# A block of three token mixers on one core: eighteen chunks of x's projections by Strassen's product, memory attention moved beside the forgetting attention's values

## The chip, the core and the metric

The kernel runs on one core of one Trainium2 chip. The metric is the device time in microseconds (us); lower is better. The engines are called as the profile calls them: PE is TensorE's matmul, DVE VectorE, ACT ScalarE, POOL GpSimd, SP the engine that issues most of the DMAs.

## The reference

One layer on x of 1024 tokens x 1024 channels in fp32. All three mixers read one combined projection of the normalised x.

```python
h = rmsnorm(x, norm_mix_g)
z = h @ w_in                                   # hq hf hi hg | fq fk fv ff | mq | 3 x 1024 gate logits
y_a = hgrn2(hq, hf, hi, hg)                    # 4 heads of 128, gated recurrence, norm per head
y_b = fox(fq, fk, fv, ff)                      # 8 heads of 64, causal attention with log-forget bias
mem_kv = rmsnorm(mem) @ mem_kv_w               # 256 memory tokens
y_c = memory(mq, mem_kv)                       # 4 heads of 128: softmax(q k') v over 256 tokens
g = sigmoid(gate_logits)                       # one gate per channel and branch
merged = g0 * (y_a @ w_br_hgrn) + g1 * (y_b @ w_br_fox) + g2 * (y_c @ w_br_mem)
x = x + merged @ w_out
a, v = split(rmsnorm(x) @ w_up)                # 2 x 2816
x = x + (gelu(causal_conv3(a) + b) * v) @ w_down
```

The square sum of a token's channels scales a whole column of x, so the kernel multiplies the raw, gain-scaled x into the weights and applies 1/rms afterwards (`rx`, the row spread over 128 partitions, or `rt`, a column per 128 tokens).

## The kernel before, in words

Data lie channel-major: a tile is 128 channels x 1024 tokens. Every large product is made of fp32r parts: an operand is cast to a high part (`uh`, `wh`, usually on ACT, L115) and the difference is the low part (`ul`, `wl`, on DVE, L123); `mm3` (L109 to L111) issues three matmuls, high x high, high x low, low x high. PSUM has eight banks of 512 columns: three named `pp` for projections, two `lg` for logits, two `tr` for transposes, one `po` for attention's sums.

The stages, in the order of time: the front (keys and values of memory, x loaded chunk by chunk and split, the first two gate chunks, the norm of x); the values of the forgetting attention (`fox_values`) and the projections of its first head pair (`fox_proj(0)`); its eight heads, two per pair p, while projections of the next pair and gate chunks are woven between; the HGRN values, preparation and mix per head; memory attention with its own projections; the three branches' output projections with the gates (`gates`); w_out; the up-projection, made by Strassen's product in units of two 128-channel chunks (84 matmuls of 512 columns where 96 would do it directly); the down-projection.

A chunk (`cm_chunk`) is 128 output channels by 1024 tokens: 48 matmuls of 512 columns. 28 such chunks are concerned here, 24 of gate logits and four of the memory's queries `mq`. A gate chunk ends in a product with `rx` on DVE (L373), a tanh on ACT (L374) and a store to memory (`gd`), from where the branches read it back. How many gate chunks are woven beside which head stands in two tables:

```python
NGF = [0, 3, 1, 2, 0, 5, 2, 0]     # beside the eight heads of the forgetting attention
NG = [1, 1, 0, 3, 0, 0, 0, 3]      # beside four HGRN heads and four memory heads
```

`weave` takes steps of several generators in turn, by the share of their steps done; `ahead` gives attention a higher priority. From that a planner writes a fixed order for each engine, with its own estimate of times; each engine then runs its list strictly in order and waits where an operand is late.

In one attention head a block of 128 queries goes through logits (PE into `lg`), a fused bias and row maximum (DVE L527), exponential (ACT L537), reciprocal (DVE L538), scaling (POOL L539), transposes (PE L550 to L553 into `tr`), the split of the transposed block (ACT L115, DVE L123: `ph`, `pl`), and the products with the values (PE L562, L563 into `po`). The end of an HGRN head's half (L727 to L749) is: `po`, its square on ACT (L741), the sum on DVE (L742), the power on POOL (L128), scaling on ACT (L745), four transposes (L748), the output `ya` on DVE (L749).

## Time and profile before

| | |
|---|---|
| median of 3 runs | 1778.67 us (1777.25 to 1780.26) |
| the profiled execution | 1779.33 us, its span from first to last instruction 1777.6 us |
| granted clock of PE | 0.997 |
| PE, DVE, ACT, POOL busy | 1755.8, 1146.1, 731.0, 359.9 us |

By stages, in us of the span, busy time of PE, DVE and ACT:

| stage | from - to | PE | DVE | ACT |
|---|---|---|---|---|
| front | 0 - 66 | 53.0 | 52.3 | 31.4 |
| values, first projections | 66 - 136 | 70.0 | 16.7 | 22.9 |
| forgetting attention | 136 - 510 | 374.0 | 225.1 | 193.0 |
| HGRN | 510 - 787 | 277.0 | 200.2 | 108.2 |
| memory attention | 787 - 884 | 97.0 | 46.6 | 44.8 |
| branches | 884 - 1020 | 136.0 | 77.6 | 26.3 |
| w_out | 1020 - 1128 | 108.0 | 64.0 | 47.8 |
| up-projection | 1128 - 1558 | 427.1 | 335.7 | 185.5 |
| down-projection | 1558 - 1777 | 213.8 | 127.9 | 71.2 |

Lines of a timeline give the start, the busy time, engine, line of the kernel, operation, output and inputs, shape, and in brackets the idle time before it with what ended it. Lines of groups end in busy time, mean duration of one in ns, and idle time before them with its causes. Busy times of neighbours overlap, since instructions are pipelined: how far two starts lie apart is the price of one.

### The profile page before, as it was taken

Reading aid. Unit: us, or ns where it says so; the run is one execution under the profiler, and the core shown is the slowest. Engines: PE = TensorE matmul, PEld = TensorE weight load, DVE = VectorE, ACT = ScalarE, POOL = GpSimd, SP = SyncE. Lnnn points to the kernel's source line nnn. Section 1 sums busy time; section 2 is a strip of 40 time slices with the busy share of each in tenths; the row PEclk is TensorE's granted clock in tenths of the full one; section 3 lists DMA queues with packets and bytes.
Section 4 is the critical chain, followed back from the end, with each engine's and each line's share of the span. In section 5 each row is a group of like instructions: output and inputs, shape, how many; then the busy total and the mean of one; then the engine's idle time right before and its main releaser. Section 6 shows DMA issues by size and latency. Waiting matters only on the chain.

```text
span 1777.6 us, 24366 instructions
## 1 busy us (share of the span) xinstructions
PE 1755.8 (99%) x9173; PEld 1487.1 (84%) x9173; DVE 1146.1 (64%) x2070; ACT 731.0 (41%) x1215; POOL 359.9 (20%) x430
## 2 busy tenths in 40 slices
PE   7999999999999999999999999999999999999999
PEld 5899899889988888888888888788888888778887
DVE  8436665565657778735446665787877877775654
ACT  4336454444544344314521143543433444433332
POOL 5214334342223333323100000111111111100000
PEclk9999999999999999999999999999999999999999
DMA  7212221221211111130144442455545444394782
GB/s 265 98 61 70 70 69 62 73 88 60 69 50 43 42 48 34 45 125 25 54 142 142 148 166 84 142 165 173 154 132 158 124 125 140 135 371 144 232 281 83
DMA packets 75573, 208.45 MB, mean 117 GB/s; under 512 B 8752, under 2 KB 11576, under 8 KB 75328
## 3 DMA queue, kind: packets, MB, share of 16 engines
q1 hardware_dynamic: 60864, 154.99, 25.2%
q0 software_dynamic: 14592, 51.91, 10.3%
q8 instruction: 72, 1.18, 0.3%
q14 instruction: 45, 0.37, 0.1%
HBM read 168.82 MB, written 61.12 MB: 129 GB/s over the span
## 4 chain that ended last, share of the span: by engine, by line
PE 96%; issue 1%; DMA 1%; DVE 1%; POOL 1%; ACT 0%; SPq 0%; DVEq 0%; POOLq 0%
PE pp L110 21%; PE pp L111 21%; PE pp L109 21%; PE lg L110 4%; PE lg L111 4%; PE lg L109 4%; PE tr L109 2%; PE tr L110 2%; PE tr L111 2%; PE lg L696 2%; PE po L563 1%; PE lg L522 1%; PE po L562 1%; PE lg L521 1%; PE po L110 1%
## 5 line engine op out<-in xcount | busy, mean ns | idle before, releaser
L111 PE MATMUL pp<-uh,wl 128*128 128x512 f32 x608 | 243.6, 401 | 0.0
L110 PE MATMUL pp<-ul,wh 128*128 128x512 f32 x608 | 243.2, 400 | 0.0
L109 PE MATMUL pp<-uh,wh 128*128 128x512 f32 x608 | 241.7, 397 | 0.0
L110 PE MATMUL pp<-wl,uh 128*128 128x256 f32 (+1 forms) x512 | 144.9, 283 | 0.0
L111 PE MATMUL pp<-wh,ul 128*128 128x256 f32 (+1 forms) x512 | 144.6, 283 | 0.0
L109 PE MATMUL pp<-wh,uh 128*128 128x256 f32 (+1 forms) x512 | 143.9, 283 | 0.0
L115 ACT CAST wh<-raw 128x1024 fp32r<-128x1024 f32 (+2 forms) x80 | 73.1, 914 | 153.0 <-PE pp L110 123.3
L109 PEld LDWEIGHTS pp<-uh,wh 128*128 128x128 f32 x608 | 115.3, 190 | 23.3
L110 PEld LDWEIGHTS pp<-ul,wh 128*128 128x128 f32 x608 | 114.5, 188 | 22.9
L111 PEld LDWEIGHTS pp<-uh,wl 128*128 128x128 f32 x608 | 114.4, 188 | 22.5
L1074 POOL DMA_DIRECT2D rw<-in_w_up x44 | 24.3, 559 | 463.8 <-DVE wl L123 410.8
L123 DVE TENSOR_TENSOR wl<-raw,wh 128x1024 fp32r<-128x1024 f32 (+2 forms) x87 | 93.9, 1081 | 29.7 <-ACT wh L115 23.0
L115 ACT CAST wh<-s 128x512 fp32r<-128x512 f32 x85 | 51.9, 619 | 125.6 <-PE pp L110 60.7
L110 PEld LDWEIGHTS pp<-wl,uh 128*128 128x128 f32 x512 | 96.4, 188 | 0.9
L111 PEld LDWEIGHTS pp<-wh,ul 128*128 128x128 f32 x512 | 96.5, 189 | 0.6
L109 PEld LDWEIGHTS pp<-wh,uh 128*128 128x128 f32 x512 | 96.2, 189 | 0.7
L115 ACT CAST dwh<-wr 128x1024 fp32r<-128x1024 f32 (+1 forms) x42 | 41.1, 980 | 124.7 <-PE tr L110 41.7
L115 ACT CAST wh<-rw 128x512 fp32r<-128x512 f32 x65 | 40.0, 620 | 86.1 <-PE pp L110 48.3
L123 DVE TENSOR_TENSOR dwl<-wr,dwh 128x1024 fp32r<-128x1024 f32 (+1 forms) x42 | 47.6, 1133 | 38.7 <-ACT dwh L115 37.5
L677 POOL TENSOR_TENSOR X<-X,kt 128x256 f32<-128x256 f32 x48 | 48.2, 1011 | 109.9 <-ACT X L676 109.9
L539 POOL TENSOR_SCALAR pt<-pt,st 128x128 f32<-128x128 f32 (+3 forms) x64 | 57.0, 891 | 62.4 <-DVE st L538 50.5
L537 ACT ACTIVATE pt<-pt,st 128x128 f32<-128x128 f32 (+3 forms) x64 | 49.7, 777 | 35.1 <-DVE st L534 29.0
(426 smaller groups left out, 4845.1 us busy)
## 6 DMA issues: line engine op xcount, KB each, us to landing
rw<-in_w_up POOLq DMA_DIRECT2D x44, 512.0 KB, 4.7
raw<-in_w_cm SPq DMA_DIRECT2D x40, 512.0 KB, 3.5
sd<-in_w_dn POOLq DMA_DIRECT2D x30, 512.0 KB, 6.1
br<-yd SPq DMA_DIRECT2D x30, 512.0 KB, 5.4
gd<-gt SPq DMA_DIRECT2D x46, 256.0 KB, 2.0
gt<-gd SPq DMA_DIRECT2D x46, 256.0 KB, 2.7
...
```

The costliest lines, as they stand in the source:

```text
L109: PE.matmul(ps, lh, rh, start=first, stop=False, skip_group_check=more)
L110: PE.matmul(ps, lh, rl, start=False, stop=False, skip_group_check=more)
L111: PE.matmul(ps, ll, rh, start=False, stop=last, skip_group_check=more)
L115: S.copy(out, in_)
L123: return (sub or V).tensor_sub(l, src, h.bitcast(F32))
L521: PE.matmul(ps[:, :w], qa[i][:, tsl], kh[i][:, s0:s0 + w], start=True, stop=False)
L522: fox_sets[p][3] = PE.matmul(ps[:, :w], qa[i][:, tsl], kl[i][:, s0:s0 + w], start=False, stop=True)
L537: S.activation(pt[:, :ns], pt[:, :ns], AF.Exp, bias=st[:, 2:3], accum_out=st[:, 3:4])
L539: G.tensor_scalar(pt[:, :ns], pt[:, :ns], st[:, 3:4], 0.0, ALU.mult, ALU.add)
L677: G.tensor_mul(Xk, Xk, Kv[:, :, 0, :])
L696: PE.matmul(o[:, b * 64:(b + 1) * 64], X[:, b * P:(b + 1) * P], Xq[:, b * bpb:(b + 1) * bpb, :], start=True, stop=True)
L1074: late["raw"] = G.dma_start(raw[:, 2 * i:2 * i + 2, :], src[:, 2 * i:2 * i + 2, :])
```

## The change

18 of the 28 chunks (the four of `mq` and 14 of the gates) are made right after the front, in nine pairs, by Strassen's product in Winograd's form: seven products of quarter size, 84 matmuls instead of 96 per pair. For that, x is read again from memory in eight loads (`rows`), scaled by the norm's gain on ACT, and sums of its quarters are split into four families T1 to T4 (`differences`), the other three operands being quarters of the parts of x that exist (B11, B21, B22). The pairs' weights come as a new input `w_pair` through POOL's queue. Two plain gate chunks (NCOVER) run before. `rx` is spread behind the last of the row loads. The results of `mq` go to memory.

Memory attention now reads them and is woven beside `fox_values` and `fox_proj(0)`; its output parts go to memory (`ycd`) and come back before the third branch. Beside the heads of the forgetting attention six gate chunks are left, two beside the second head of each of the first three pairs (NFOX). Beside the first three HGRN heads only the next head's preparation is woven, beside the last the branch of the forgetting attention (`branch(1)`); then follow the branches of HGRN and of memory. Sums and parts of the branches lie in the place of x's parts.

```diff
-NGF = [0, 3, 1, 2, 0, 5, 2, 0]
-NG = [1, 1, 0, 3, 0, 0, 0, 3]
-NPRE = 2 + sum(NG) + sum(NGF)
+ORDER = [(br, j) for br in (1, 0, 2) for j in range(8)]
+NCOVER, NPAIR, NFOX = 2, 14, 2
+
+_dense = [12, 13, 14, 15] + [16 + 8 * br + j for br, j in ORDER[4:4 + NPAIR]]
+PAIRS = list(zip(_dense[0::2], _dense[1::2]))
+assert 2 + NCOVER + NPAIR + 3 * NFOX == len(ORDER) and len(_dense) % 2 == 0
...
+    early = iter([i for i in range(2, len(order)) if i < 2 + NCOVER or i >= 2 + NCOVER + NPAIR])
+
+    def gates_early(count):
+        for _ in range(count):
+            i = next(early)
+            br, j = order[i]
+            for n, ps in cm_chunk(w_cm[16 + 8 * br + j], KC, uh, ul):
+                SP.dma_start(gd[i, n], gate(n, ps))
+                yield
...
+    def block(b, k):
+        if b in fam:
+            return [t[:, k, :] for t in fam[b]]
+        c, n = int(b[1]) - 1, int(b[2]) - 1
+        return [t[k + 4 * c][:, n * HB:(n + 1) * HB] for t in (uh, ul)]
+
+    def product(ps, op, b, first):
+        wh, wl = op
+        for k in range(4):
+            ks = slice(k * P, (k + 1) * P)
+            bh, bl = block(b, k)
+            mm3(ps, wh[:, ks], wl[:, ks], bh, bl, first and k == 0, k == 3, not first)
...
+        def snap(self, ps):
+            e = ps1.tile([P, HB], F32, tag="fe", name="fe", bufs=3)
+            S.copy(e, ps)
+            return e
...
+    def dense_unit(src, put, first, families):
+
+        raw = []
+        whole = None if first else dense.raw()
+        for i in range(2):
+            if first:
+                t = wp.tile([P, 4 * 264], F32, tag="raw", name="raw", bufs=2)[:, :2 * HB]
+                t = t.rearrange("p (a b) -> p a b", a=2)
+            else:
+                t = whole[:, 2 * i:2 * i + 2, :]
+            G.dma_start(t, src[:, 2 * i:2 * i + 2, :])
+            raw += [t[:, 0, :], t[:, 1, :]]
+        a11, a21, a22, a12 = raw
+        x, y = ps_proj(), ps_lg()
+        o1 = dense.operand(a11)
+        if first:
+            o6 = dense.operand(a12)
+        s1 = dense.sum_of(1, a21, a22)
+        o2 = dense.operand(s1)
+        s2 = dense.sum_of(2, s1, a11)
+        product(x, o1, "B11", True)
+        e1 = dense.snap(x)
+        if first:
+            z = ps_tr()
+            product(z, o6, "B21", True)
+            put(0, 0, z, e1)
+            next(families)
+        product(y, o2, "T1", True)
+        e5 = dense.snap(y)
+        product(x, dense.operand(s2), "T2", False)
+        e2 = dense.snap(x)
+        run_all(families)
+        s4 = dense.sum_of(4, s2, a12)
+        product(y, dense.operand(s4), "B22", False)
+        put(0, 1, y, e2)
+        s3 = dense.sum_of(3, a11, a21)
+        product(x, dense.operand(s3), "T3", False)
+        put(1, 1, x, e5)
+        if not first:
+            z = ps_tr()
+            product(z, dense.operand(a12), "B21", True)
+            put(0, 0, z, e1)
+        product(x, dense.operand(a22), "T4", False)
+        put(1, 0, x, None)
...
+            if e is not None:
+                V.tensor_add(t, ps, e)
+            src = ps if e is None else t
+            if c:
+                V.scalar_tensor_tensor(out=t, in0=src, scalar=-1.0, in1=rx[:, sl], op0=ALU.mult, op1=ALU.mult)
+            else:
+                V.tensor_mul(t, src, rx[:, sl])
+            S.activation(t, t, AF.Tanh, scale=0.5)
+            SP.dma_start(gd[order.index(divmod(ch - 16, 8)), n], t)
...
+    for k, t in enumerate(rows):
+        t = t.rearrange("p (c n) t -> p c (n t)", c=2)
+        for c in range(2):
+            last_row = SP.dma_start(t[:, c, :], xT[:, k + 4 * c, :])
+    with tc.issue_after(last_row.ins):
+        spread_dma(rx, rt, cp, "rx")
...
+    def differences():
+
+        b = []
+        for k, t in enumerate(rows):
+            t = t.rearrange("p (c n) t -> p c (n t)", c=2)
+            for c in range(2):
+                S.activation(t[:, c, :], t[:, c, :], AF.Copy, scale=col(C_GX + k + 4 * c))
+            b.append([t[:, c, n * HB:(n + 1) * HB] for c in range(2) for n in range(2)])
+        for k, (b11, b12, b21, b22) in enumerate(b):
+            V.tensor_sub(b11, b11, b12)
+            family_block("T1", k, b11)
+        yield
+        order_after = ExitStack()
+        order_after.enter_context(tc.issue_after(first_gates.ins))
+        for k, (t1, b12, b21, b22) in enumerate(b):
+            V.scalar_tensor_tensor(out=t1, in0=t1, scalar=-1.0, in1=b22, op0=ALU.mult, op1=ALU.subtract)
+            family_block("T2", k, t1)
...
+    cover, families = gates_early(NCOVER), differences()
+    next(cover)
+    next(families)
+    run_all(cover)
+    next(families)
+    for i, chunks_of in enumerate(PAIRS):
+        dense_unit(w_pair[i], dense_put(chunks_of), i == 0, families)
+    ps1.release()
+    fam.clear()
...
+    def mem_prep(h):
+        mqh = pm.tile([P, T], F32R, tag="mqh", name=f"mqh_{h}", bufs=2)
+        mql = pm.tile([P, T], F32R, tag="mql", name=f"mql_{h}", bufs=2)
+        rq = pm.tile([P, 8], F32, tag="rq", name=f"rq_{h}", bufs=2)
+        t = pm.tile([P, T], F32, tag="mqf", name=f"mqf_{h}", bufs=2)
+        SP.dma_start(t, mqd[h])
...
+            for t, d in zip(yt, ycd):
+                SP.dma_start(d[:, h, n * HB:(n + 1) * HB], t.bitcast(F32))
+            yield
+
+    def memory():
+        run_all(mem_prep(0))
+        yield
+        for h in range(4):
+            if h < 3:
+                run_all(mem_prep(h + 1))
+            yield from mem_attn(h)
...
-    run_all(fox_values())
+    weave((chain(fox_values(), fox_proj(0)), 25), (ahead(memory(), AHEAD), 4 * MEM_STEPS))
     small_consts()
-    run_all(fox_proj(0))
+    pm.release()
+    pf = pools["pf"] = tc.alloc_tile_pool(name="pf", bufs=1, side="right", reuse_waits="tile")
+    mskf = pf.tile([P, P], F32, tag="mskf", name="mskf")
+    SP.dma_start(mskf, mats[:, 2 * P:3 * P])
     fox_prep(0)
     for p in range(3):
-        weave((ahead(fox_attn(p, 0), AHEAD), FOX_STEPS), (fox_proj(p + 1), 8),
-              (gates_early(NGF[2 * p]), 2 * NGF[2 * p], FOX_LATE))
+        weave((ahead(fox_attn(p, 0), AHEAD), FOX_STEPS), (fox_proj(p + 1), 8))
         fox_prep(p + 1, fox_sets[p][3])
-        weave((ahead(fox_attn(p, 1), AHEAD), FOX_STEPS),
-              (gates_early(NGF[2 * p + 1]), 2 * NGF[2 * p + 1], FOX_LATE))
+        weave((ahead(fox_attn(p, 1), AHEAD), FOX_STEPS), (gates_early(NFOX), 2 * NFOX, FOX_LATE))
...
-        weave((ahead(fox_attn(3, i), AHEAD), FOX_STEPS), (islice(values, 8), 8),
-              (gates_early(NGF[6 + i]), 2 * NGF[6 + i], FOX_LATE))
+        weave((ahead(fox_attn(3, i), AHEAD), FOX_STEPS), (islice(values, 8), 8))
...
-        weave((ahead(hgrn_mix(h, ya), AHEAD), HGRN_STEPS), (hgrn_prep(h + 1), 6), (gates_early(NG[h]), 2 * NG[h]))
-    weave((ahead(hgrn_mix(3, ya), AHEAD), HGRN_STEPS), (gates_early(NG[3]), 2 * NG[3]))
+        weave((ahead(hgrn_mix(h, ya), AHEAD), HGRN_STEPS), (hgrn_prep(h + 1), 6))
...
+    yh, yl = [[place(p, 2 + c, f"y{p}{c}") for c in range(4)] for p in "hl"]
+    for c in range(4):
+        t = place("hl"[c % 2], c // 2, f"yb{c}", F32)
+        SP.dma_start(t, ybd[:, c, :])
+        split(S, yh[c], yl[c], t)
...
+    weave((ahead(hgrn_mix(3, ya), AHEAD), HGRN_STEPS), (branch(1, yh, yl), 16))
+    state["ph"].release()
+    pv.release()
+    for c in range(4):
+        split(S, yh[c], yl[c], ya[:, c, :])
+    py = tc.alloc_tile_pool(name="py", bufs=1, side="right", reuse_waits="tile")
+    yc = [[py.tile([P, T], F32R, tag=f"yc{p}{c}", name=f"yc{p}{c}") for c in range(4)] for p in "hl"]
+    for c in range(4):
+        for t, d in zip(yc, ycd):
+            G.dma_start(t[c], d[:, c, :].bitcast(F32R))
+    run_all(branch(0, yh, yl))
+    run_all(branch(2, *yc))
```

How the planner's order changes is shown at three places. Line numbers behind the change are about 280 higher in the attention and HGRN. The first is ACT at the end of the front; `rx_row` is the row of 1/rms, `Vf` the attention's values. Before:

```order
L115 CAST wh_763<-raw_761 128x1056
L276 COPY rx_row_499<-tr_497 8x128
L420 ACTIVATE Vf_529<-pp_553,rt_88 128x256
L420 ACTIVATE Vf_529<-pp_579,rt_88 128x256
L374 ACTIVATE gt_510<-gt_510 128x512
L374 ACTIVATE gt_514<-gt_514 128x512
L374 ACTIVATE gt_518<-gt_518 128x512
L420 ACTIVATE Vf_529<-pp_605,rt_88 128x256
```

Now, with `xrT4h`, `rw`, `xrT4l` the row tiles, `T1h` the high part of family T1, `s1`, `s2` sums of the first pair's weights:

```order
L119 CAST wh_722<-raw_716 128x512
L119 CAST wh_722<-raw_718 128x512
L280 COPY rx_row_535<-tr_533 8x128
L548 ACTIVATE xrT4h_512<-xrT4h_512,cv_64 128x1024 x2
L119 CAST T1h_516<-xrT4h_512 128x512
L548 ACTIVATE rw_514<-rw_514,cv_64 128x1024 x2
L119 CAST T1h_516<-rw_514 128x512
L548 ACTIVATE xrT4l_513<-xrT4l_513,cv_64 128x1024 x2
L119 CAST wh_730<-s1_728 128x512
L119 CAST wh_730<-s2_734 128x512
L119 CAST T1h_516<-xrT4l_513 128x512
L548 ACTIVATE rw_515<-rw_515,cv_64 128x1024 x2
```

Where the values' evictions and the gates' tanh stood behind the copy of `rx_row`, eight scales of rows and the casts of T1 and of two operands now stand.

The second is PE in the last head of the forgetting attention, at its last rows of logits (`kh1_3`, `qa1_3`). Before, with `pp_5416` the projection of the HGRN values:

```order
L109 MATMUL pp_5416<-wh_5139,uh0_71 128x256
L551 MATMUL tr_5374<-ident_65,pt_5329 128x128
L551 MATMUL tr_5387<-ident_65,pt_5329 128x128
L550 MATMUL tr_5374<-ident_65,pt_5313 128x128
L550 MATMUL tr_5387<-ident_65,pt_5313 128x128
L551 MATMUL tr_5374<-ident_65,pt_5329 128x128
L551 MATMUL tr_5387<-ident_65,pt_5329 128x128
L521 MATMUL lg_5468<-kh1_3_3859,qa1_3_3861 128x512
L522 MATMUL lg_5468<-kl1_3_3863,qa1_3_3861 128x512
L110 MATMUL pp_5416<-wl_5140,uh0_71 128x256
L111 MATMUL pp_5416<-wh_5139,ul0_72 128x256
L109 MATMUL pp_5416<-wh_5139,uh1_73 128x256
```

Now, with `po_7051` the next to last block's output:

```order
L830 MATMUL tr_7065<-ident_65,pt_6991 128x128
L831 MATMUL tr_7052<-ident_65,pt_7007 128x128
L831 MATMUL tr_7065<-ident_65,pt_7007 128x128
L801 MATMUL lg_7142<-kh1_3_5857,qa1_3_5859 128x512
L802 MATMUL lg_7142<-kl1_3_5861,qa1_3_5859 128x512
L801 MATMUL lg_7146<-kh1_3_5857,qa1_3_5859 128x512
L802 MATMUL lg_7146<-kl1_3_5861,qa1_3_5859 128x512
L842 MATMUL po_7051<-ph_7057,vhl_6309 128x256
L830 MATMUL tr_7078<-ident_65,pt_6991 128x128
L831 MATMUL tr_7078<-ident_65,pt_7007 128x128
L833 MATMUL tr_7078<-ident_65,pt_7007 128x128
L843 MATMUL po_7051<-pl_7058,vhl_6309 128x256
```

Between the last logits and the products with the values there are no projections any more; the projections for HGRN come before or behind.

The third is PE at the end of the last HGRN head (`po` its output, `tr` its transposes). Before:

```order
L729 MATMUL po_7793<-St_7800,qe_7745 128x128
L727 MATMUL po_7793<-Vf_529,A_7629 128x128
L111 MATMUL pp_7889<-uh6_83,wl_7886 128x512
L109 MATMUL pp_7889<-uh7_85,wh_7885 128x512
L110 MATMUL pp_7889<-ul7_86,wh_7885 128x512
L729 MATMUL po_7793<-St_7804,qe_7745 128x128
L111 MATMUL pp_7889<-uh7_85,wl_7886 128x512
L109 MATMUL pp_7922<-uh0_71,wh_7885 128x512
L110 MATMUL pp_7922<-ul0_72,wh_7885 128x512
L111 MATMUL pp_7922<-uh0_71,wl_7886 128x512
```

Now, with `pp_9588`, `pp_9589` and `pp_9628` sums of a branch on the parts `yh3`:

```order
L1010 MATMUL po_9442<-St_9203,qe_9415 128x128
L1008 MATMUL po_9442<-Vf_2030,A_9228 128x128
L1010 MATMUL po_9442<-St_9445,qe_9415 128x128
L1008 MATMUL po_9442<-Vf_2030,A_9228 128x128
L1010 MATMUL po_9442<-St_9449,qe_9415 128x128
L1008 MATMUL po_9442<-Vf_2030,A_9228 128x128
L1010 MATMUL po_9442<-St_9453,qe_9415 128x128
L1029 MATMUL tr_9467<-ident_65,o2_9457 128x128 x4
L113 MATMUL pp_9588<-yh3_8934,wh_9584 128x512
L113 MATMUL pp_9589<-yh3_8934,wh_9584 128x512
L113 MATMUL pp_9628<-yh3_8934,wh_9624 128x512
L114 MATMUL pp_9588<-yl3_8938,wh_9584 128x512
```

Where matmuls of a projection stood between and behind the last `po` matmuls, the transposes now follow directly, and behind them come matmuls that read the branch's last parts.

342 lines of the change are left out of this document (183 added, 159 removed).

## The prediction

> **What bounds the kernel now.** I read the summary by engines first, then the chain of waits, then the table by stretches, and last the timeline around the few gaps that TensorE (PE) has. Span, busy time and chain:
>
> ```profile
> core 0: 1777.6 us, clock 0.997
> PE 1755.8 (99%) x9173; PEld 1487.1 (84%) x9173; DVE 1146.1 (64%) x2070; ACT 731.0 (41%) x1215; POOL 359.9 (20%) x430
> PE 96%; issue 1%; DMA 1%; DVE 1%; POOL 1%; ACT 0%; SPq 0%; DVEq 0%; POOLq 0%
> ```
>
> PE is busy for 99% of the span at nearly full clock, and 96% of the chain that ends last is PE. So a matmul taken away shortens the kernel by its issue interval, as long as PE still finds its next operand ready; and a stretch in which PE has to wait lengthens it at once, since there is no slack to absorb it. The stretches tell how little it waits now, and the price of a matmul (time, then busy time and instructions of PE, PEld, DVE, ACT, POOL, clock, DMA):
>
> ```profile
> 136.00:510.00 374.00, 374.00 (x2471) 340.43 (x2470) 225.12 (x662) 192.97 (x371) 133.54 (x172) 1.00 0.21 70
> 575.00:635.00 60.00, 60.00 (x343) 51.26 (x342) 46.94 (x95) 23.69 (x46) 21.30 (x20) 1.00 0.12 42
> 1132.00:1554.00 422.00, 419.40 (x1815) 340.58 (x1814) 328.55 (x490) 179.29 (x272) 61.82 (x99) 1.00 0.50 146
> ```
>
> From 136 to 510 (the forgetting attention with projections and gate chunks woven in) PE never stops; in the HGRN stage VectorE (DVE) is busy 46.9 of 60 us and PE still never stops. From 1132 to 1554 is the up-projection, already by Strassen's product: 419.4 us for 1815 matmuls of 512 columns, 0.231 us each. Its one gap, and one in the down-projection, show what a wait costs beside itself:
>
> ```profile
> 1137.38 0.51 PE L109 MATMUL pp<-T3h,wh 128*128 128x512 f32 x1 [2.60 <-ACT wh L115]
> 1141.18 0.63 PE L109 MATMUL pp<-T3h,wh 128*128 128x512 f32 x1
> 1141.61 0.60 PE L110 MATMUL pp<-T3l,wh 128*128 128x512 f32 x1
> 1142.03 0.41 PE L111 MATMUL pp<-T3h,wl 128*128 128x512 f32 x1
> ...
> 1561.08 0.50 PE L110 MATMUL pp<-dbl,dwh 128*128 128x512 f32 x1 [1.53 <-DVE dbl L123]
> ...
> 1561.88 0.61 PE L110 MATMUL pp<-dbl,dwh 128*128 128x512 f32 x1
> 1562.29 0.63 PE L111 MATMUL pp<-dbh,dwl 128*128 128x512 f32 x1
> ...
> 1565.27 0.41 PE L111 MATMUL pp<-dbh,dwl 128*128 128x512 f32 x1
> ```
>
> After the wait of 1.53 us eight matmuls start 0.42 us apart instead of 0.231 (1561.88 to 1565.27 is 3.39 us for eight): another 3.39 - 8 x 0.231 = 1.5 us is lost. Behind the wait of 2.60 us such rows come too. So a wait of 1.5 us or more is charged about 1.6 us on top, once per place.
>
> **Part 1: the matmuls removed.** A pair of chunks takes 2 x 2 x 8 x 3 = 96 matmuls of 512 columns directly, and 7 products x 4 x 3 = 84 by Strassen. Nine pairs: 108 matmuls fewer, and no other matmul form changes its count. 108 x 0.231 = **-25.0 us**, all on the path.
>
> **Part 2: the dense units in steady state.** One unit is 84 x 0.231 = 19.4 us of PE. Its casts, sums and splits are those of a unit of the up-projection, where 1815/84 = 21.6 units needed 328.55 us of DVE, 15.2 each, and 8.3 of ScalarE (ACT), without a gap after the first. The dense unit has no depthwise convolution, so it needs less. **0**; the work of 19.4 us on PE covers it.
>
> **Part 3: the start of the dense stage.** Eight rows of x are read again, scaled on ACT, subtracted and split into the family T1 before the first T1 product. The front's end on PE, then the row prices: four of the front, and two averages over the up-projection:
>
> ```profile
> 66.17 0.28 PE L109 MATMUL pp<-wh,uh 128*128 128x256 f32 x1
> 55.97 1.07 ACT L267 ACTIVATE xk<-xk 128x1024 f32<-128x1024 f32 x1 [2.56 <-DVE ul L265]
> 67.76 0.26 ACT L276 COPY rx_row<-tr 8x128 f32<-8x128 f32 x1 [7.46 <-PE tr L274]
> 73.10 1.29 DVE L373 TENSOR_TENSOR gt<-lg,rx 128x512 f32<-128x512 f32 x2 [10.65 <-DMA rx<-rx_d]
> 74.31 0.68 DVE L373 TENSOR_TENSOR gt<-pp,rx 128x512 f32<-128x512 f32 x1
> L115 ACT CAST wh<-s 128x512 fp32r<-128x512 f32 x85 | 51.9, 619 | 125.6 <-PE pp L110 60.7 <-PE lg L110 33.0 <-PE tr L110 21.3
> L123 DVE TENSOR_TENSOR wl<-s,wh 128x512 fp32r<-128x512 f32 x85 | 58.2, 685 | 4.9 <-ACT wh L115 4.9
> ```
>
> ACT's order puts the eight scales behind the copy of rx_row, which ends at 68.0 and, with the cover's matmuls ahead of its transpose, about 1.3 later: 69.3. Each of four blocks then costs ACT two scales (2.14), the wait for DVE's subtraction (0.69) and the cast of T1h (0.62), 3.45 us; with two casts of weights (1.24) T1 is cast at 69.3 + 13.8 + 1.2 = 84.3. DVE's split (0.69) and the first gate (0.69), which stands behind it and frees the lg bank of the first T1 product, end at 85.7. PE has until then two half chunks of the cover and B21 of the first unit, 24 + 24 + 12 matmuls, 13.9 us from the front's end at 66.2 (the first matmul of the values): it runs dry at about 80.2. Wait 5 us, slow rows 1.6, and two changes of product on one PSUM bank (B11, T2, T3) that wait for ACT's snapshot (0.62 and an eviction's latency, 0.9 each): **+9**, bounds 7 (the wait alone a little longer) to 12 (rows land late as well: eight loads of 512 KB).
>
> **Part 4: forgetting attention with fewer fillers.** Before, 13 gate chunks were woven between its heads, now 6, and none for heads 0, 2, 4, 6 and 7; the planner's fixed order leaves three stretches where PE has attention alone: 8.3, 14.4 and 6.8 us of PE work. What these engines then need, from the stage before:
>
> ```profile
> L123 DVE TENSOR_TENSOR pl<-tr,ph 128x512 fp32r<-128x512 f32 x48 | 32.2, 685 | 14.9 <-ACT ph L115 14.8
> L527 DVE CUSTOM_DVE_ANT_0 pt<-lg,nf 128x512 f32<-128x512 f32 x32 | 22.0, 688 | 19.1 <-PE lg L522 10.3 <-PE tr L550 8.5
> L527 DVE CUSTOM_DVE_ANT_0 pt<-lg,nfm 128x128 f32<-128x128 f32 x64 | 18.3, 286 | 13.9 <-POOL nfm L516 6.8 <-PE tr L553 2.9 <-PE tr L550 2.4
> L123 DVE TENSOR_TENSOR pl<-tr,ph 128x384 fp32r<-128x384 f32 x32 | 17.6, 549 | 2.1 <-ACT ph L115 2.0
> L567 DVE TENSOR_TENSOR yp<-po,yp 64x256 f32<-64x256 f32 x32 | 13.2, 412 | 5.4 <-ACT yp L566 5.4
> L534 DVE TENSOR_SCALAR st<-st 128x1 f32<-128x1 f32 x56 | 11.5, 206 | 0.7
> L538 DVE RECIPROCAL st<-st 128x1 f32<-128x1 f32 x64 | 10.3, 161 | 32.6 <-ACT pt L537 32.5
> L115 ACT CAST ph<-tr 128x512 fp32r<-128x512 f32 x48 | 27.1, 588 | 20.0 <-PE tr L551 10.7 <-PE po L562 8.9
> L537 ACT ACTIVATE pt<-pt,st 128x1024 f32<-128x1024 f32 x8 | 9.2, 1150 | 7.7 <-DVE st L534 7.7
> L539 POOL TENSOR_SCALAR pt<-pt,st 128x1024 f32<-128x1024 f32 x8 | 9.0, 1125 | 10.2 <-DVE st L538 10.2
> ```
>
> In the 14.4 us stretch DVE's order holds 5 logit reductions of 512 columns, 4 of 384 or 256, 12 of 128, 7 differences of 512, 4 of 384, 5 sums into yp and 22 single-column operations: 3.4 + 2.0 + 3.4 + 4.8 + 2.2 + 2.1 + 4.1 = 22.0 us by the means. The means overlap (above, two operations of 0.68 start 1.21 apart, 0.605 each), so by 0.605/0.685 it is 19.4 us: PE cannot be faster than DVE there, a wait of at least 5.0. With the chain at its end I take **6**. The 6.8 us stretch is the last head's end and is held by a round trip: the last row of logits (two reductions of 512 columns or nearly so, 1.4), two single-column operations (0.4), exponential (1.15), reciprocal (0.16), the product on POOL (1.13), together 4.2 us before its first transpose, in which PE has only 2.0 us of the head's other products; then four groups through two tr banks, each a cast and a difference (0.59 + 0.69) behind its transposes. 2.2 + about 2 = **4**. The 8.3 us stretch holds 14 us of DVE in its order, of which only the 8.6 up to the last difference is waited for; as a chain **5**. Slow rows once, 1.6. Sum **+16.6**; bounds 10 (attention runs far enough ahead that only DVE's surplus of 5.0 and half of the rest counts) and 20 (slow rows in all three).
>
> [...] This trace has half-rate rows behind a wait of 1.53 us already, so I keep the row.
>
> **Part 5: the end of the HGRN stage.** The last mix's output ya of head 3 is now operand of the branch woven beside it (its fourth part, k=3) and of the next one; PE's order has 4 logit, 8 po and 4 transposing matmuls in sequence and then matmuls on yh3 alone. Before, 34 matmuls of projections lay between po and the transposes. The same chain in the trace:
>
> ```profile
> 777.65 0.38 PE L729 MATMUL po<-St,qe 128*128 128x128 f32 x2
> 778.12 0.60 ACT L741 ACTIVATE o<-po 128x512 f32<-128x512 f32 x1 [5.76 <-PE po L729]
> 778.76 0.69 DVE L742 TENSOR_REDUCE rr<-o 128x4 f32<-128x512 f32 x1 [5.16 <-ACT o L741]
> 779.73 1.01 POOL L128 TENSOR_TENSOR rr<-rr,mhalf 128x4 f32<-128x4 f32 x1 [7.91 <-DVE rr L127]
> 780.77 1.14 ACT L745 ACTIVATE o<-po,rr 128x128 f32<-128x128 f32 x4 [2.05 <-POOL rr L128]
> 785.77 0.60 PE L748 MATMUL tr<-ident,o 128*128 128x128 f32 x4
> 786.41 0.75 DVE L749 SCALAR_TENSOR_TENSOR ya<-tr,hgc,hz 128x512 f32<-128x512 f32 x1 [0.43 <-PE tr L748]
> ```
>
> From po to the scaled output 777.65 to 781.91, 4.3 us; transposes to ya 785.77 to 787.16, 1.4; the cast of a 1024-column part 1.05 (as the scale above) and its difference about as much, less three matmuls in between, 0.4. That is 7.1 us, plus 1.5 for the mask and the state updates between the logits and po: 8.6, and slow rows 1.9: **+10.5**, bounds 7.5 to 13.
>
> **Parts that I cost at nothing.** Memory attention beside the values: 67 us of matmuls over some 36 us of attention. Reading gates and yc back: hundreds of us ahead of their use. The weights on POOL's queue: they come a unit ahead of PE. Without cover, each would be a DMA's landing of 3 to 5 us.
>
> **Sum.** 1777.6 - 25.0 + 9 + 16.6 + 10.5 = 1788.7 span. The profiled execution was 1779.33, 1.7 over its span, and 0.7 over the median 1778.67; so 1788.7 + 1.1 = **1790 us**. All lower bounds give 1778, all upper ones 1799; three separate terms are seldom all at one end, so its own range is 1781 to 1798.
>
> **Rivals.** (a) Faster: the planner's order has the other engines ahead when a bare stretch begins, so their work there is partly done. Attention is issued at high priority, and before no stretch shows a wait; against it, DVE's 19.4 us lie in the order between PE's ends of the stretch. If this holds at a third of part 4 (5.5), and part 3's wait is halved (5) with the tail at 7.5: 1778.7 - 25 + 18 = 1771.7. It decides from waits under 25 us in all. (b) About even: the lower bounds, 7 + 10 + 7.5 = 24.5, cancel part 1: 1778. (c) The dense units bind after all, because each product waits for a snapshot or an operand's split: two such waits of 0.9 in each of nine units, 16 us more: 1806. Against it stands the up-projection with one gap in 21 units. (d) The change saves less than counted since PE issues slower: excluded by the equal matmul forms. [...]
>
> **Chances.** My forecast 0.55, (a) 0.27, (b) 0.11, (c) with the slow clock 0.07. About 0.2%, 3.6 us, is what a measurement of this kernel can tell from no change. Faster is (a) with a little of (b): 0.29; same 0.12; slower 0.59. The range 1766 to 1800 leaves out the end of (a) and (c); the forecast's own is 1781 to 1798.
>
> **What would show it.** Right: PE gaps of 4 us or more on the first T1 product, gaps of 1 to 3 us at po and tr rows of the attention between gate chunks, released by ACT or DVE, one of about 4 us before the last transposes of HGRN and one behind them; PE busy about 25 us less. Wrong: gaps of under 25 us in all, which makes it faster; gaps inside the later dense units, which makes it slower than said.

## The result and the profile after

The changed kernel takes **1795.38 us** (median; 1793.32 to 1796.05) against 1779.47 us of the kernel before beside it: 1.0089 times as long, 95% interval [1.0072, 1.0107]. It is slower by about 16 us; 1790 us had been predicted. The profile is of one execution, the lowest of the four at 1793.32 us, so some 2 us of the 16 have no place in what follows. It has a span of 1791.4 us, 13.8 us more than before. Cores, engines and the chain of waits of the changed kernel:

```profile
core 0: 1791.4 us, clock 0.991
PE 1746.6 (98%) x9065; PEld 1474.2 (82%) x9065; DVE 1214.8 (68%) x2210; ACT 783.7 (44%) x1312; POOL 379.7 (21%) x449
PE 91%; DVE 3%; issue 2%; ACT 1%; DMA 1%; POOL 1%; SPq 0%; DVEq 0%; POOLq 0%; ACTq 0%
```

PE has 108 instructions fewer, but only 9.2 us less busy time (1755.8 before), and the share of PE in the chain fell from 96% to 91%. The rest is waiting, and busy time at a lower clock. The table by stretches of the changed kernel (time, then busy time and instructions of PE, PEld, DVE, ACT, POOL, then clock, DMA) shows where:

```profile
67.10:130.00 62.90, 58.79 (x245) 46.66 (x245) 43.17 (x69) 34.34 (x54) 3.20 (x6) 0.97 0.48 178
130.00:500.00 370.00, 370.00 (x2297) 330.54 (x2296) 207.50 (x450) 181.90 (x359) 83.31 (x115) 1.00 0.26 91
500.00:720.00 220.00, 206.57 (x1396) 186.52 (x1395) 141.76 (x442) 119.02 (x236) 90.81 (x115) 0.98 0.17 56
720.00:945.00 225.00, 224.85 (x1284) 191.28 (x1283) 183.99 (x377) 98.19 (x176) 95.83 (x74) 1.00 0.17 54
945.00:990.00 45.00, 39.11 (x188) 32.06 (x187) 26.14 (x42) 7.74 (x14) 5.34 (x9) 0.92 0.60 190
```

Three stretches lose: the start of the dense stage (67 to 130), the second half of the forgetting attention (500 to 720), and the end of HGRN (945 to 990). Between 130 and 500, that is a little over seven of the nine dense units, memory attention and the first heads, PE is busy all the time. The timeline of PE has these waits there, among others:

```profile
84.15 0.47 PE L113 MATMUL lg<-T1h,wh 128*128 128x512 f32 x1 [2.76 <-DVE gt L378]
103.29 0.50 PE L113 MATMUL pp<-T2h,wh 128*128 128x512 f32 x1 [0.68 <-ACT fe L424]
...
518.53 0.39 PE L843 MATMUL po<-pl,vhl 128*128 128x256 f32 x1 [0.96 <-DVE pl L127]
...
627.48 0.50 PE L801 MATMUL lg<-kh,qa 128*128 128x512 f32 x1 [0.73 <-DVE st L807]
634.15 0.56 PE L842 MATMUL po<-ph,vhl 128*128 128x256 f32 x1 [2.08 <-ACT ph L119]
...
696.11 0.30 PE L830 MATMUL tr<-ident,pt 128*128 128x128 f32 x1 [0.91 <-DVE pl L127]
700.96 0.33 PE L831 MATMUL tr<-ident,pt 128*128 128x128 f32 x1 [2.25 <-POOL pt L819]
709.29 0.79 PE L113 MATMUL pp<-uh,wh 128*128 128x512 f32 x1 [1.51 <-DVE zt L895]
...
961.83 1.25 PE L1029 MATMUL tr<-ident,o 128*128 128x128 f32 x4 [3.16 <-ACT o L1026]
965.01 1.65 PE L113 MATMUL pp<-yh,wh 128*128 128x512 f32 x3 [1.92 <-ACT yh L119]
```

The waits of the three stretches come to 23.4 us; the lines show the longer ones. To weigh a place with all that happens there, I take for each matmul the time to the next one's start, less what its shape usually takes in the kernel before (0.232 us for 512 columns, 0.119 for 256, 0.11 for 128), and add that up over a stretch. This is the **loss** in the table below; it holds waits, a slow clock, and whatever else keeps PE from its usual pace. Differences of a few tenths mean nothing. A **slow window**, in what follows, is a stretch of 3.41 us in which the granted clock is 0.50; in the changed kernel's from 709.30 us on, matmuls of 512 columns start 0.43 us apart.

| place | before | after | term in the prediction |
|---|---|---|---|
| front, to 66.1 or 67.1 us | 13.3 | 13.5 | 0 |
| dense stage's start | -0.5 | 6.5 | +9 |
| rest to the end of the attention | -1.5 | 24.1 | +16.6 |
| HGRN up to its end | 6.7 | 6.6 | 0 |
| end of HGRN | (in the row above) | 8.8 | +10.5 |
| first 172 us or so of the up-projection, and the rest behind it | 5.2 | 2.1 | 0 |

The differences are +0.2, +7.0, +25.6, -0.1, +8.8 and -3.1: 38.4 us. With -25.0 us of matmuls that makes 13.4, and the spans differ by 13.8.

### The profile page after: what moved, and what is told of

It reads as the page before. It is cut to its first block, busy times and chain, and to the rows that moved or that the text cites. A ratio compares the mean times of both kernels' runs of the same rounds, so it can differ in the third digit from the quotient of the medians.

```text
span 1791.4 us, 24546 instructions
## 1 busy us (share of the span) xinstructions
PE 1746.6 (98%) x9065; PEld 1474.2 (82%) x9065; DVE 1214.8 (68%) x2210; ACT 783.7 (44%) x1312; POOL 379.7 (21%) x449
## 3 DMA queue, kind: packets, MB, share of 16 engines
q1 hardware_dynamic: 64464, 159.19, 25.6%
q0 software_dynamic: 18336, 65.54, 12.6%
## 4 chain that ended last, share of the span: by engine, by line
PE 91%; DVE 3%; issue 2%; ACT 1%; DMA 1%; POOL 1%; SPq 0%; DVEq 0%; POOLq 0%; ACTq 0%
PE pp L115 19%; PE pp L114 19%; PE pp L113 19%; PE lg L113 4%; PE lg L115 4%; PE lg L114 4%; PE tr L113 2%; PE tr L114 2%; PE tr L115 2%; PE lg L977 1%; PE po L843 1%; PE po L113 1%; PE po L114 1%; PE po L115 1%; PE lg L801 1%
## 5 line engine op out<-in xcount | busy, mean ns | idle before, releaser
L113 PE MATMUL pp<-uh,wh 128*128 128x512 f32 x356 | 141.8, 398 | 1.5 <-DVE zt L895 1.5
L115 PE MATMUL pp<-uh,wl 128*128 128x512 f32 x356 | 143.1, 402 | 0.0
L114 PE MATMUL pp<-ul,wh 128*128 128x512 f32 x356 | 143.1, 402 | 0.0
L119 ACT CAST wh<-s 128x512 fp32r<-128x512 f32 x121 | 73.0, 619 | 157.6 <-PE pp L114 67.1
L1254 POOL DMA_DIRECT2D rw<-in_w_up x44 | 24.1, 554 | 389.8 <-DVE wl L127 176.6
L127 DVE TENSOR_TENSOR wl<-s,wh 128x512 fp32r<-128x512 f32 x121 | 82.5, 685 | 12.0 <-ACT wh L119 12.0
L127 DVE TENSOR_TENSOR wl<-raw,wh 128x1024 fp32r<-128x1024 f32 (+2 forms) x72 | 74.1, 1030 | 14.6 <-ACT wh L119 14.3
L113 PEld LDWEIGHTS pp<-uh,wh 128*128 128x128 f32 x356 | 67.8, 190 | 15.4 <-DVE zt L895 1.6
L114 PEld LDWEIGHTS pp<-ul,wh 128*128 128x128 f32 x356 | 67.4, 189 | 14.3
L115 PEld LDWEIGHTS pp<-uh,wl 128*128 128x128 f32 x356 | 67.4, 189 | 14.0
L127 DVE TENSOR_TENSOR wl<-rw,wh 128x512 fp32r<-128x512 f32 x89 | 59.7, 687 | 27.0 <-PE pp L115 12.3
```

Source lines behind the costliest of these rows:

```text
L113: PE.matmul(ps, lh, rh, start=first, stop=False, skip_group_check=more)
L114: PE.matmul(ps, lh, rl, start=False, stop=False, skip_group_check=more)
L115: PE.matmul(ps, ll, rh, start=False, stop=last, skip_group_check=more)
L119: S.copy(out, in_)
L127: return (sub or V).tensor_sub(l, src, h.bitcast(F32))
L1254: late["raw"] = G.dma_start(raw[:, 2 * i:2 * i + 2, :], src[:, 2 * i:2 * i + 2, :])
```

## The experiments

In each, the time beside the name is the median, with the ratio to the kernel before. Losses by place are made as above, each from one profiled execution, which can lie up to 4 us off the median of its kernel.

### The dense stage without Strassen's product

```diff
...
-    for i, chunks_of in enumerate(PAIRS):
-        dense_unit(w_pair[i], dense_put(chunks_of), i == 0, families)
+    for ch in _dense:
+        for n, ps in cm_chunk(w_cm[ch], KC, uh, ul):
+            if ch < 16:
+                t = gate_tile()
+                S.copy(t, ps)
+                SP.dma_start(mqd[ch - 12][:, n * HB:(n + 1) * HB], t)
+            else:
+                SP.dma_start(gd[order.index(divmod(ch - 16, 8)), n], gate(n, ps))
```

> The changed kernel, but the 18 chunks of the dense stage are computed plainly (48 matmuls each, after the two cover chunks) instead of by Strassen's product; rows, families and paired weights are left out. Everything behind the stage stays. Theory (each removed matmul is worth its issue interval, steady units cost nothing, the stage's start costs 6.5 us): 108 more matmuls x 0.232 = +25.0, the start's 6.5 us gone, so 1795.4 + 25.0 - 6.5 = 1814 us, and the three waits in the forgetting attention (4.6, 9.7 and 10.8 us) and the one at the end of HGRN (8.9) remain. Rival (the units bind in part, so Strassen's product saves less than 25): below 1805.

Measured: 1813.7 us, 1.0197 [1.0176, 1.0217], as the theory had it. The stretch of the dense stage's start in this kernel:

```profile
67.00:130.00 63.00, 63.00 (x274) 51.16 (x274) 16.19 (x17) 16.75 (x24) 3.01 (x2) 1.00 0.37 132
```

PE never waits there and the loss is 0.0; the attention loses 26.1 and the end of HGRN about 9, much as in the changed kernel. So Strassen's product saves 25 us less 6.5 for its start, 18.3 net between the two kernels, and the steady units cost nothing. What made the kernel slower lies in the rearrangement: it would have been 35 us slower with the same order and plain products.

### Fewer pairs, more gate chunks beside the attention

```diff
-NCOVER, NPAIR, NFOX = 2, 14, 2
+NCOVER, NPAIR = 2, 8
+NGF = [0, 3, 1, 2, 0, 4, 2, 0]
...
+              (gates_early(NGF[2 * p]), 2 * NGF[2 * p], FOX_LATE))
...
```

The second kernel has instead:

```diff
+NCOVER, NPAIR = 2, 12
+NGF = [0, 2, 0, 2, 0, 3, 1, 0]
...
```

> The changed kernel with six pairs instead of nine by Strassen's product (four chunks of mq, eight of the gates) and twelve gate chunks woven beside the forgetting attention (0, 3, 1, 2, 0, 4, 2, 0 beside its eight heads) instead of six. In PE's order no bare stretch of more than 2.5 us is left there. Theory (the 25 us lost in the attention come from the bare stretches alone): 36 more matmuls, +8.4, less 25: 1795.4 + 8.4 - 25 = 1779 us, with the loss at HGRN's end still there. Rival (attention waits because of something else that the change brought, such as more DMA traffic): the waits stay and the time is 1795 to 1804.

Measured: 1784.05 us, 1.0033 [1.0021, 1.0045], 11 us less than the changed kernel with 36 matmuls more. The attention's second half:

```profile
510.00:720.00 210.00, 208.16 (x1295) 185.52 (x1293) 126.14 (x360) 103.28 (x197) 69.29 (x87) 0.99 0.21 70
```

PE waits 1.8 us there, where it waited 13.4 us in 500 to 720; the loss of the attention fell from 24.1 to 3.4 us. The waits came from the bare stretches; that there are fewer pairs isn't what ended them, since with no pairs at all the attention had lost 26.1. The time is 5 us above the 1779 that the theory gave, for two reasons: 3.4 were left instead of none, and the loss at the end of HGRN rose, which no theory had foreseen. Counted in both kernels from 30 us ahead of the last transposes, it went from 9.5 to 12.6 us. PE has two waits there that the changed kernel doesn't have, 0.62 us for a part of the branch (`yl`) and 0.92 for DVE's `A`; why they came was not followed.

> As the kernel with six pairs, but with eight pairs (12 gate chunks dense) and eight gate chunks beside the attention (0, 2, 0, 2, 0, 3, 1, 0). PE's order then has bare stretches of 8.6, 6.1 and 5.3 us instead of 8.6, 14.8 and 6.9. Theory (the loss grows with a stretch's length and with the slow clock windows behind it): 12 more matmuls, +2.8; the first stretch loses 4 to 5 us as before, the middle one 3 to 4 instead of 9.7, the last 8 to 10: about 1795.4 + 2.8 - 7 = 1791 us. Rival (each stretch costs a fixed round trip whatever its length): 1797 or more.

Measured: 1793.07 us, 1.0081 [1.0060, 1.0101]. The loss of the attention is 15.9 us, 8 less than in the changed kernel. About 5 of it is new and lies earlier, at 269 us: PE waits 2.06 us for ACT's squares of the memory's queries, ACT for the load of these queries, and two slow windows follow. So the bare stretches themselves lose some 11 us instead of 25: 4.1, 1.7 and 5.0 instead of 4.6, 9.7 and 10.8. The time lies between the two theories' figures (1791 and 1797); the places decide. The first stretch kept its length and its loss, and the middle one, less than half as long, lost a fifth, so a stretch has no fixed price. The last one shrank only from 6.9 to 5.3 us and lost half all the same: its waits fell from 5.8 to 3.3 us, and neither of the two slow windows came. About 3 us of the gain were lost again at the end of HGRN (12.3 instead of 9.5, counted as above).

### Another branch behind HGRN

```diff
-    run_all(branch(0, yh, yl))
     run_all(branch(2, *yc))
+    run_all(branch(0, yh, yl))
```

> The changed kernel with the last two branches exchanged: the memory branch, whose operand lies in memory, runs ahead of the HGRN branch, which needs ya of the last head. Theory (the loss of 8.9 us at the end of HGRN is the round trip from the last po to yh3, with nothing else to do for PE): matmuls of the memory branch fill it as far as its loads have landed; 4 to 8 us less, 1788 to 1791 us. Rival (that branch's loads wait for the same tiles to come free, so PE waits for them instead): 1795 or more.

Measured: 1802.76 us, 1.0132 [1.0115, 1.0149]: the rival, and worse than it said. At the end of HGRN:

```profile
960.39 1.25 PE L1029 MATMUL tr<-ident,o 128*128 128x128 f32 x4 [3.16 <-ACT o L1026]
964.10 1.65 PE L113 MATMUL pp<-ych,wh 128*128 128x512 f32 x3 [2.46 <-DMA ych<-ychd]
```

The wait before the transposes is unchanged, and behind it PE waits for the memory branch's operand from memory, whose loads could only start when HGRN's tiles were free (they are issued at 959.9 to 964.0 us). Moreover the HGRN branch's matmuls on heads 0 to 2, which had been cover ahead of the last po, were gone from there: PE waits 0.57 and 1.57 us ahead of the last po, and five slow windows follow each other. The loss at this place rose from 8.8 to about 16.

### Filling the end of HGRN

```diff
+        if (br, j) == (0, 1):
+            ps = [ps_lg(), ps_lg()]
+            with tc.issue_after(late["po"].ins):
+                for n in range(2):
+                    for k in range(3):
+                        mm3(ps[n], wh[:, k, :], wl[:, k, :], yh[k][:, half[n]], yl[k][:, half[n]], k == 0, False)
+            for n in range(2):
+                mm3(ps[n], wh[:, 3, :], wl[:, 3, :], yh[3][:, half[n]], yl[3][:, half[n]], False, True)
...
```

> The changed kernel; only the second chunk of the HGRN branch is summed in the two lg banks instead of pp banks, and its first 18 matmuls, which read the parts of heads 0 to 2, are put in PE's order between the last po matmul and the last four transposes. The work is the same. Theory (the 8.9 us at the end of HGRN are two waits of 3.2 and 1.9 us without other work, and slow clock windows behind them): 18 x 0.232 = 4.2 us of matmuls fill the first wait, five matmuls on the high parts stand in front of the second one; the loss falls from 8.9 to 2 to 4 us, so 1789 to 1791 us. Rival (the wait is set by DVE's or POOL's chain, and the chain is delayed by as much as is filled, or the matmuls only move from a place where they were cover themselves): 1794 or more.

Measured: 1796.08 us, 1.0091 [1.0076, 1.0106]: no gain. The wait of 3.16 us before the transposes is gone, but these two are there:

```profile
966.31 0.73 PE L113 MATMUL pp<-yh,wh 128*128 128x512 f32 x2 [1.92 <-ACT yh L119]
...
979.47 0.50 PE L113 MATMUL pp<-yh,wh 128*128 128x512 f32 x1 [2.17 <-DVE gt L1105]
```

The second is new: once yh3 is there, five banks of sums end at once, and the next chunk waits for DVE to merge them with their gates. The loss at this place is 7.2 instead of 8.8.

```diff
-        split(S, yh[c], yl[c], ya[:, c, :])
+        for sl in ([slice(0, HB), slice(HB, T)] if c == 3 else [slice(0, T)]):
+            split(S, yh[c][:, sl], yl[c][:, sl], ya[:, c, sl])
```

> The changed kernel, but the parts yh, yl of HGRN's last head are cast in two halves of 512 tokens, so that the first half doesn't wait for the end of the last mix. Theory (at the end of HGRN PE lacks matmuls that are free of the last half): sums of the first half can finish and leave their bank, and 9 matmuls stand in PE's order between the last po and the transposes; the loss falls from 8.9 to 3 to 5 us, 1790 to 1792 us. Rival (what the matmuls fill here they leave open just before, where the mix waits for DVE): the loss moves to the 20 us ahead, 1794 or more.

Measured: 1793.53 us, 1.0086 [1.0071, 1.0101]. The same place in this kernel:

```profile
970.95 1.10 PE L1029 MATMUL tr<-ident,o 128*128 128x128 f32 x4 [0.68 <-ACT o L1026]
973.55 0.96 PE L113 MATMUL pp<-yh,wh 128*128 128x512 f32 x3 [1.50 <-ACT yh L119]
986.27 0.50 PE L113 MATMUL pp<-yh,wh 128*128 128x512 f32 x1 [1.72 <-DVE gt L1096]
```

The first wait fell to 0.68 us and the loss to 6.2. HGRN ahead of it lost about 3 more in this execution (9.8 instead of 6.6), but not in the 20 us ahead, as the rival has it: it lies at 729 to 737 us, in waits of 0.37, 0.50 and 0.67 us and one slow window. The kernel with four cover chunks below has the same there, so the halved cast is not its cause. A median lower by 1.9 us is within what the measurement can tell. Both fillings shift waits rather than end them: the round trip through DVE, POOL and ACT is shown to be the first cause, since matmuls put beside it shorten the wait before the transposes, and the merges behind it are the next.

### The start of the dense stage

```diff
-NCOVER, NPAIR, NFOX = 2, 14, 2
...
+NCOVER, NPAIR, NFOX = 4, 12, 2
+
+_dense = [12, 13, 14, 15] + [16 + 8 * br + j for br, j in ORDER[2 + NCOVER:2 + NCOVER + NPAIR]]
```

> The changed kernel with eight pairs instead of nine, whose two chunks run plainly ahead of the dense stage: four cover chunks instead of two. 12 more matmuls, +2.8. Theory (the start of the dense stage loses 2.8 us in a wait for T1 and 1.7 in a slow clock window behind it, because the cover is too short; the two waits of 0.7 for the snapshots don't depend on it): -4.5, so 1795.4 + 2.8 - 4.5 = 1794 us, and no wait before the first T1 product. Rival (the wait is for something that the cover delays too, the gates' products and banks): the wait stays, 1798 us.

Measured: 1803.99 us, 1.0134 [1.0119, 1.0150]. The rival holds:

```profile
85.29 0.79 PE L113 MATMUL pp<-uh,wh 128*128 128x512 f32 x1 [6.54 <-DVE gt L378]
```

PE doesn't even get to the first T1 product: the third half chunk of the cover waits 6.54 us for a pp bank. At this time four banks (two lg, one pp, one po) hold the first gate chunks and two more the cover's results, and none is let go of until DVE has multiplied it by rx, which stands behind the splits of T1. Cover needs pp banks, and there are none. In the kernel with plain products, where no splits stand before the gates, such chunks ran here without a wait. The loss at this place is 9.1 instead of 6.5. That is not all of the 8.6 us by which the median rose: 2.8 are the matmuls, and about 3 more were lost at 735 to 744 us, at the start of HGRN, to three short waits and a slow window.

```diff
-                S.activation(t[:, c, :], t[:, c, :], AF.Copy, scale=col(C_GX + k + 4 * c))
+                if c:
+                    G.tensor_scalar(t[:, c, :], t[:, c, :], col(C_GX + k + 4 * c), 0.0, ALU.mult, ALU.add)
+                else:
+                    S.activation(t[:, c, :], t[:, c, :], AF.Copy, scale=col(C_GX + k + 4 * c))
```

> The changed kernel, but of the eight scales of x's rows at the start of the dense stage four run on POOL and four on ACT, instead of all on ACT. Theory (the wait of 2.8 us before the first T1 product ends with the first gate's product, which stands on DVE behind the splits of T1; these follow ACT's chain of eight scales, four casts and two more, which can start only when rx_row is copied): the chain is 4 x 1.05 = 4.2 us shorter, T1 and the first gate are ready at about 80, before PE's cover ends at 81; the wait and the slow clock window behind it go, about 4 us: 1791 to 1792 us. Rival (the gate waits for rx, whose write to memory stands behind the row loads on their way): the wait stays at 2 us or more, 1794 to 1796 us.

Measured: 1794.96 us, 1.0089 [1.0074, 1.0105], loss at this place 6.3. No gain, though not for the reason of the theory's rival either: rx landed at 79.3 us, 3.7 ahead of the first gate's product. In the changed kernel one block of the chain to T1 looks like this:

```profile
70.19 2.19 ACT L548 ACTIVATE xrT4h<-xrT4h,cv 128x1024 f32<-128x1024 f32 x2
71.37 0.69 DVE L551 TENSOR_TENSOR xrT4h<-xrT4h 128x512 f32<-128x512 f32 x1 [5.36 <-ACT xrT4h L548]
72.29 0.60 ACT L119 CAST T1h<-xrT4h 128x512 fp32r<-128x512 f32 x1
72.79 2.19 ACT L548 ACTIVATE rw<-rw,cv 128x1024 f32<-128x1024 f32 x2
```

and here, with the later wait on ACT as its last line:

```profile
70.00 1.15 ACT L551 ACTIVATE xrT4h<-xrT4h,cv 128x1024 f32<-128x1024 f32 x1
71.91 0.62 ACT L119 CAST T1h<-xrT4h 128x512 fp32r<-128x512 f32 x1 [0.76 <-DVE xrT4h L554]
72.43 1.15 ACT L551 ACTIVATE rw<-rw,cv 128x1024 f32<-128x1024 f32 x1
78.22 1.14 ACT L119 CAST wh<-s 128x512 fp32r<-128x512 f32 x2 [2.21 <-PE pp L114]
```

T1 takes both its operands from the first of a block's two scales (`b11` and `b12` in the code), the one that stayed on ACT. In the changed kernel DVE's subtraction ran beside ACT's second scale; here ACT stands 0.76 us until it is done. So a block takes 2.43 us instead of 2.60, and the four scales that went to POOL were no part of the way to T1. Then ACT, in order, stands 2.21 us instead of 0.83 at two casts of weights that need a buffer which PE still reads, with the third of T1's casts behind them. T1's last split ends at 83.0 instead of 83.4. The row loads don't pace this: the rows of the later blocks landed at 70.1, 72.7 and 75.2, at least 2.2 us before ACT took them up.

### Combinations

Four kernels put the findings together. They are made of the edits above, with these numbers, the second with the lower two lines, the others with the upper two:

```diff
+NCOVER, NPAIR = 2, 8
+NGF = [0, 3, 1, 2, 0, 4, 1, 1]
...
+NCOVER, NPAIR = 4, 6
+NGF = [0, 3, 1, 2, 0, 3, 2, 1]
```

> The kernel with six pairs and twelve gate chunks beside the attention (now 0, 3, 1, 2, 0, 4, 1, 1, so that the last head has one too), and the filled end of HGRN. By the theory's sum, losses added to the matmuls' gain: -36 x 2 x 0.232 = -16.7 (72 matmuls fewer than the kernel before), +6.4 at the dense stage's start, +1 to 2 in the attention, +2 to 4 at the end of HGRN: 1778.9 - 16.7 + 11 = 1773 us, faster than the kernel before. Rival (there is a loss that the sum by places leaves out, such as a slower front or up-projection): 1779 or more.

Measured: 1784.04 us, 1.0023 [1.0014, 1.0032]. The rival's figure: the filling gains nothing here either. 12.6 us are lost at the end of HGRN, counted from 30 us ahead of the last transposes, though only 3.4 in the attention.

> Five pairs by Strassen's product (60 matmuls fewer than the kernel before, -13.9 us), four cover chunks, twelve gate chunks beside the attention (0, 3, 1, 2, 0, 3, 2, 1), and the filled end of HGRN. Theory: 1778.9 - 13.9 + 1.9 (snapshots and little else at the dense stage's start) + 0 to 1 in the attention + 2 to 4 at the end of HGRN = 1768 to 1771 us, below the kernel with six pairs, since 4.5 us of losses go for 2.8 us of matmuls. Rival (a chunk more in the cover only moves the wait): 1774 or more.

Measured: 1786.3 us, 1.0038 [1.0026, 1.0049]. Both hopes failed: the four cover chunks lose 9.1 us at the dense stage's start as above, where 1.9 had been put down, and the end of HGRN loses 10.9 instead of 2 to 4.

> Six pairs by Strassen's product, twelve gate chunks beside the attention (0, 3, 1, 2, 0, 4, 1, 1), scales shared by POOL and ACT, the halved cast and the filled end of HGRN (second chunk of the branch in the lg banks). From the measured kernel with six pairs and the filled end, 1784: less 4 at the dense stage's start, less 3 to 5 at HGRN's end, 1775 to 1777 us: about 0.2% below the kernel before. Rival (the slow clock windows, which fall by chance of where a wait lies, give back what the waits leave): 1779 to 1781 us.

Measured: 1783.73 us, 1.0026 [1.0016, 1.0035]. It gained nothing on the first either: the wait before T1 is still 2.59 us, and the end of HGRN loses 11.5, 4.46 of it a wait for DVE's merges. So it is also above the rival's figure. The fourth has the numbers of the first, the shared scales and the halved cast, and puts the two casts behind T1's (`family_block` returns the cast on ACT here):

```diff
+            late["t1"] = family_block("T1", k, b11, True)
...
+            with tc.issue_after(late["t1"].ins):
+                o2 = dense.operand(s1)
...
```

> Six pairs by Strassen's product and twelve gate chunks beside the attention (0, 3, 1, 2, 0, 4, 1, 1), scales of x's rows shared by POOL and ACT, the casts of the first pair's two weight sums put behind the four casts of T1 in ACT's order, and the parts of HGRN's last head cast in halves (the branch's banks as in the change). Theory, as formed from the runs so far (T1 is late because ACT, in order, holds two casts in the middle of T1's chain that wait until PE has let go of a weights' buffer, at 78.2; then the first gate stands behind T1's splits): without them the four blocks of 2.4 us each end at 79.7, two splits of weights and the first gate at about 82; PE waits 1 to 1.4 us instead of 2.6, too short for a slow clock window, 3 us gained at this place; at HGRN's end 2 to 3 us less than with the whole cast. 1784 - 5 = 1779 us, even with the kernel before. Rival (the first gate waits for rx, which lands after its way through memory): the wait stays at 2 us or more, 1782 to 1784 us.

Measured: 1781.48 us, 1.0011 [1.0002, 1.0020]. Of the two reasons for 1779 us one held, since the end of HGRN loses 10.0 instead of 12.6, and one failed: the wait before T1 is still there. On PE:

```profile
84.43 0.47 PE L114 MATMUL lg<-T1h,wh 128*128 128x512 f32 x1 [2.95 <-DVE gt L379]
```

and on POOL, DVE and ACT before it (two splits of weights stand on DVE from 82.39 on):

```profile
71.35 1.12 POOL L563 TENSOR_SCALAR rw<-rw,cv 128x1024 f32<-128x1024 f32 x1 [1.43 <-DMA rw<-in_xT]
71.46 1.55 DVE L568 TENSOR_TENSOR xrT4h<-xrT4h 128x512 f32<-128x512 f32 x1 [5.30 <-ACT xrT4h L565]
73.04 0.62 ACT L405 CAST T1h<-xrT4h 128x512 fp32r<-128x512 f32 x1 [1.62 <-DVE xrT4h L568]
76.61 1.47 DVE L406 TENSOR_TENSOR T1l<-rw,T1h 128x512 fp32r<-128x512 f32 x1 [0.69 <-ACT T1h L405]
81.79 0.69 DVE L406 TENSOR_TENSOR T1l<-rw,T1h 128x512 fp32r<-128x512 f32 x1 [0.68 <-ACT T1h L405]
83.60 0.69 DVE L379 TENSOR_TENSOR gt<-lg,rx 128x512 f32<-128x512 f32 x1
```

The weights' casts no longer block ACT, yet T1 ends at 82.5, since ACT waits for DVE's subtraction in each of the four blocks, 1.62, 1.24, 1.07 and 0.76 us; the first two subtractions took 1.55 and 1.17 us instead of 0.69. The gate that lets go of the lg bank then stands behind two splits of weights as well. That the gate's place in DVE's order is what ends the wait, the releaser shows in every kernel that has it. An earlier gate was not tried. rx would not have held it back: it landed at 79.3 us, and PE ran dry at 81.5. What the wait of about 2.7 us would need to vanish stays open. No kernel is faster than the one before.

## Why the prediction was right

It was slower, by 16 us where 11 had been forecast, at the three places and in the main for the reasons given; two terms were too large, one too small. That it isn't further off is partly luck: part 4 was 9.0 us short, while parts 3 and 5 and the up-projection were 6.8 long together. Of the signs of being right two failed: the wait on the first T1 product was 2.76 us, not 4 or more, and PE's busy time fell by 9.2 us, not by about 25.

**Part 1, -25.0.** Right: the kernel with plain products was 18.3 us slower than the changed one, 25.0 less the loss of 6.5 that it doesn't have.

**Part 2, 0.** Right: loss of -0.7 from 130 to 500 us. Rival (c), units that bind at 1806, falls with it.

**Part 3, +9.** 7.0. The end of the chain was described rightly: the wait ended with the first gate behind T1's splits on DVE, a slow window followed, then two waits of 0.68 for the snapshot. For these 0.9 each had been put down, 0.62 of it from a row; the rest, an eviction's latency, no run shows. Mis-sized was the first wait, 2.76 for 5. PE began this stage 1 us later than assumed, and T1 was cast at 82.7 instead of 84.3, although ACT's chain began 0.9 later than assumed. The 0.69 us per block in which ACT was to wait for DVE's subtraction were not there, because the subtraction runs beside the second scale: the blocks start 2.60 us apart, not 3.45. Too little cover, which I took for the cause, was only half of it: with more cover PE waits for banks instead.

**Part 4, +16.6.** This is the step that failed in size: 25.6. By the three places the losses are 4.6 (5 predicted), 9.7 (6) and 10.8 (4), and the slow rows, counted once there, came three times inside these. For the last head I took 2.2 for its round trip and "about 2" for the groups behind it. The waits in it are 0.91, 2.25, 0.40, 0.33 and two of 0.21, 4.3 together, so that was right; but two slow windows fell on it, and behind it came a wait of 1.51 for a bank of HGRN's first projection that I hadn't followed. This last wait is the one that stays with twelve gate chunks too. That DVE bounds the middle stretch is borne out only in part. Its reductions end waits of 0.57 and 0.73 us, but it is busy for 10.3 of the 14 us from 622 to 636. The longest wait, 2.08, ends with ACT's cast of ph, which stands behind two exponentials of 1.04 and 1.13 us while DVE itself waits for them.

**Part 5, +10.5.** 8.8: a wait of 3.16 before the transposes, 0.81 before the first po and 1.92 before the first matmul on yh3, and two slow windows; the waits of 5.9 stand against the 8.6 that were worked out (its parts add up to 7.4 and 1.5, not 7.1 and 1.5, and the 1.5 came from no row), and the slow windows cost more than the 1.9 put down.

Not in the sum: -3.1 in the up- and down-projections, whose waits of 2.60 and 1.53 are unchanged, but weren't followed by a slow clock in this execution. That is chance, as the last section shows.

Of the parts costed at nothing, one was described wrongly without harm: the loads of yc were not issued hundreds of us ahead of their use but at 961 to 966 us, some 40 ahead, and their median landing took 6.8 us (`ych`) and 7.6 (`ycl`) where 3 to 5 had been put down. With the branches exchanged this is what PE waits for, 2.46 us.

Rival (a) was to decide from waits of under 25 us in all, and that mark was wrong. PE's idle time rose from 21.8 to 44.8 us, by 23.0, and the kernel is slower all the same, since 15.8 of the 25.0 us that the matmuls should have taken from its busy time came back as slower pace. What counts is the loss, 41 us at the three places. The mechanism of (a), other engines far ahead when a bare stretch begins, falls with the attention's 25.6 us. Rival (b), the lower bounds, would have needed 10 there. The slow clock that the chances put with (c) came as three windows of 3.41 us in the attention, whose bare stretches are 29.5 us by part 4 (8.3, 14.4 and 6.8).
